# Offsets of split weights in SBUF, PSUM banks cleared by VectorE, and the order and stores at the end of an encoder trunk

## The chip, the cores and the metric

The kernel runs on one core of a Trainium2 chip. The metric is the device time of one execution in microseconds, the median of three runs.

## The reference

One layer of a streaming encoder on x of 256 tokens by 2048 channels, all in float32, with a memory of 256 tokens:

```
h = rms_norm(x, norm_mix_g);  x = x + hybrid_mixer(h, ...)      # w_in: 2048 x 18464, w_out: 2048 x 2048
h = rms_norm(x, norm_x_g);    x = x + cross_attention(h, mem_n, w_xq, w_xkv, w_xo)
h = rms_norm(x, norm_ffn_g);  x = x + square(relu(h @ w_ff1)) @ w_ff2     # 2048 x 8192 and 8192 x 2048
out = rms_norm(x, norm_final_g)
```

The mixer holds two recurrences over chunks of 64 tokens (retention and gated DeltaNet); their arithmetic is small beside the projections, which read 391 MB from HBM in this kernel, scratch included.

## The kernel before

**Products in three parts.** TensorE (PE) multiplies in a short float format (`fp32r`), so each operand is split in two: ACT copies the float32 data into a high part, and DVE subtracts that from the data for a low part. A product of two matrices is high x high + high x low + low x high. Activations stand in tiles `q`, a high and a low half side by side; weights come by DMA into `raw` (1 MB a piece, issued on SP's queue) and are split by `fetch` into `whi` and `wlo` (L93 and L94), 128 x 1024 each, in four buffers.

**Three ways to use them.** `chunk` (token-major projections) loads activations as the stationary operand and streams 512 columns of weights past them (L134 to L136). `blocks` (feature-major projections: the result has channels on the partitions) does the reverse: for each of 16 slices of the contraction, 128 x 128 blocks of `whi` are loaded and the 512 columns of the high and low activations streamed past (L172, one matmul for each of two banks), and then blocks of `wlo`, past which only the 256 columns of high activations are streamed (L174). These four matmuls, two wide and two narrow, are called a pass here. `seven_products` does part of the second MLP product by Strassen's scheme with seven instead of eight products: stationary `q` or `cm` (mixes of hidden activations), streams `sh` and `sl` of 256 columns (mixed weights; L1043 to L1045, 42 matmuls a call, 16 calls: `strassen(q)` for q = 0 to 3 in each of the four blocks `fb` of the MLP). The seven results accumulate over the whole MLP in four PSUM banks `seven`, which `unmix` reads at the end. `thin` is a small form of `blocks`.

**Places in SBUF.** A tile can be used from an offset within its room: `SHIFT` = 48 elements = 192 bytes. In the built program, before and after the change alike, every `q`, `whi`, `wlo`, `sh`, `sl` and `cm` begins 224 bytes past a multiple of 256, so that the offset in the code is the distance, within 256 bytes, between what a matmul streams and what is loaded meanwhile. `chunk` uses offset 0. `blocks` calls `fetch` with `at=SHIFT`, so `whi` and `wlo` both stand at +192. `seven_products` takes its offset from the call: 8 x ((4 fb + q) mod 8) elements, 0, 32, ... 224 bytes, each for two of the 16 calls.

**Order.** The code is written in program order, and a scheduler reorders it by priority: `tc.high_priority(offset=...)` draws a part ahead (fetches by 100000, evacuations by 50000). Each engine then executes its list in order. In the MLP, each `fb` has eight `blocks` (hidden activations, w_ff1), among which `strassen(0)` and `strassen(1)` follow, then three `chunk`s n = 1, 2, 3 (w_ff2), after each of which but the last comes the next `strassen`. `unmix` follows the chunk n = 2 of the last `fb`. The very last chunk is given `hold`: the weights of its two last quarters are fetched early into tiles `q`. Its evacuation `evac_last` normalises each row and stores it.

**The banks `seven`** are opened for accumulation by a matmul with a matrix of zeros, `none` (L1002). The last 128 tokens are written out by four stores of 128 x 512 on SP's queue (L1137); ACT scales the columns c = 0 and 1 (L1136), DVE c = 3 and 2 (L1132, L1134), in the order c = 0, 3, 1, 2.

Of the kernel before, what the change touches and what calls it, by code (L numbers as in the profile page):

```python
# [11 lines left out]
F32R = mybir.dt.float32r  # L12
I32 = mybir.dt.int32
AF = mybir.ActivationFunctionType
# [3 lines left out]
P = 128  # L18
# [15 lines left out]
SHIFT, ROOM = 48, 64  # L34
# [16 lines left out]
def trunk(ctx: ExitStack, tc: tile.TileContext, x, mem, positions, norm_mix_g, w_in, conv_w, gdn_a_log, gdn_dt_bias,  # L51
# [23 lines left out]
    def fetch(pieces, k, n, rush=False, hold=None, at=0):  # L75

        raw = wp.tile([P, k * n], F32, name="raw", tag="raw", bufs=3)
        rv = raw.rearrange("p (k n) -> p k n", k=k)
        with tc.high_priority(offset=100000):
            for off, ap in pieces:  # L80
                src = ap.rearrange("(k p) n -> p k n", p=P)
                for ks in ((slice(0, k // 2), slice(k // 2, k)) if rush else (slice(0, k),)):
                    nc.sync.dma_start(rv[:, ks, off:off + ap.shape[1]], src[:, ks, :])
            got = []
            for i in range(2):
                if hold:
                    both = hold().both
                    hi, lo = (both[:, a:a + 2, :].rearrange("p a s -> p (a s)") for a in (0, 2))
                else:
                    hi, lo = (wp.tile([P, 1024 + ROOM], F32R, name=e, tag=e, bufs=4)[:, at:at + k * n // 2]  # L90
                              for e in ("whi", "wlo"))
                src = raw[:, i * k * n // 2:(i + 1) * k * n // 2]
                act.activation(hi, src, AF.Copy)  # L93
                vec.tensor_sub(lo, src, hi.bitcast(F32))  # L94
                got.append((hi.rearrange("p (k n) -> p k n", n=n), lo.rearrange("p (k n) -> p k n", n=n)))
        return got
# [58 lines left out]
    def cols(w, c0, n=512):  # L155
        return lambda q: [(0, w[q * 512:(q + 1) * 512, c0:c0 + n])]

    def blocks(quads, w, c0, nb, evac, whole=None):

        k = 16 // nb
        ps = stream_ps()
        n = nb * P
        for g in range(KT // k):
            halves = fetch([(0, w[g * k * P:(g + 1) * k * P, c0:c0 + n])], k, n, at=SHIFT)
            for i in range(k):
                kk = g * k + i
                xh, xhl = quads[kk // 4][0][:, kk % 4, :], quads[kk // 4].both[:, kk % 4, :]
                wh, wl = (a[:, i % (k // 2), :] for a in halves[i // (k // 2)])  # L170
                for b in range(nb):
                    pe.matmul(ps[b], wh[:, b * P:(b + 1) * P], xhl, start=kk == 0, stop=False)  # L172
                for b in range(nb):
                    pe.matmul(ps[b][:, :S], wl[:, b * P:(b + 1) * P], xh, start=False, stop=kk == KT - 1)  # L174
        if whole:
            with tc.high_priority(offset=50000):
                o = whole()
                for b in range(nb):
                    act.activation(o[:, b, :], ps[b][:, S:], AF.Copy)
                    vec.tensor_add(o[:, b, :], o[:, b, :], ps[b][:, :S])  # L180
                evac(o)
            return
        for b in range(nb):
            with tc.high_priority(offset=50000):
                o = sm.tile([P, S], F32, name="bo", tag="bo", bufs=2)
                act.activation(o, ps[b][:, S:], AF.Copy)  # L186
                vec.tensor_add(o, o, ps[b][:, :S])  # L187
                evac(b, o)
# [704 lines left out]
    def residual_pass(quads, w, gain, name, loader=None):  # L893
        nxt = []
        acc = xa.tile([P, S], F32, name="acc2", tag="acc2", bufs=2)
        vec.memset(acc, 0.0)
        for b2 in range(8):
            xc = loader(b2) if loader else None
            if b2 % 2 == 0:
                nxt.append(quad_b())  # L900

            def evac(b, ps):
                k = 2 * b2 + b
                vec.tensor_add(rt[:, k, :], ps, xc[:, b, :] if loader else rt[:, k, :])
                g = gains[:, gain + k:gain + k + 1]
                qh, ql = (a[:, k % 4, :] for a in nxt[-1])
                act.activation(qh, rt[:, k, :], AF.Copy, scale=g)
                vec.scalar_tensor_tensor(ql, rt[:, k, :], g, qh.bitcast(F32), op0=ALU.mult, op1=ALU.subtract)
                sq = xa.tile([P, S], F32, name="sq2", tag="sq2", bufs=2)
                act.activation(sq, rt[:, k, :], AF.Square)  # L910
                vec.tensor_add(acc, acc, sq)

            blocks(quads, w, b2 * 256, 2, evac)
        ps = bank()
        for t in range(NT):
            pe.matmul(ps[:, 2 * t:2 * t + 2], acc[:, t * P:(t + 1) * P], ones[:, :2], start=True, stop=True)
        s = sm.tile([P, NT], F32, name=f"{name}_s", tag="rc_s")
        vec.tensor_scalar(s, ps[:, 0:4:2], 1.0 / D, EPS, op0=ALU.mult, op1=ALU.add)
        r = cp.tile([P, NT], F32, name=f"{name}_r")
        rsqrt(r, s)  # L920
        return nxt, r
# [74 lines left out]
        pe.matmul(rps[:, t * P:(t + 1) * P], rstd3[:, t:t + 1].to_broadcast([P, P]), ident, start=True, stop=True)  # L996
    act.activation(rrow3, rps[:, :S], AF.Copy)
    seven = [bank() for _ in range(4)]
    none = fp.tile([P, P], F32R, name="none", bufs=1)
    act.activation(none, ident, AF.Copy, scale=0.0)  # L1000
    for g in range(4):
        pe.matmul(seven[g], none, h3[g].both[:, 0, :], start=True, stop=False)  # L1002

    def mixes(hs):

# [7 lines left out]
        vec.tensor_sub(cm[:, 1], cb, cm[:, 0].bitcast(F32))  # L1013
        return cm

    def seven_products(both, cm, src, last, at):

        raw = wp.tile([P, 2048], F32, name="raw", tag="raw", bufs=3)
        rv = raw.rearrange("p (i x c) -> p i x c", i=2, x=4)
        tt = fp.tile([P, 2, 4, 256], F32, name="tt", tag="tt", bufs=1)  # L1020
        with tc.high_priority(offset=100000):
            nc.sync.dma_start(raw.rearrange("p (k n) -> p k n", k=4), src.rearrange("(k p) n -> p k n", p=P))
            vec.tensor_add(tt[:, :, 0:2, :], rv[:, :, 0:1, :].to_broadcast([P, 2, 2, 256]), rv[:, :, 1:3, :])  # L1023
            vec.tensor_add(tt[:, :, 2, :], tt[:, :, 1, :], rv[:, :, 1, :])
            vec.tensor_add(tt[:, :, 3, :], tt[:, :, 2, :], rv[:, :, 3, :])  # L1025
        for i in range(2):
            with tc.high_priority(offset=100000):
                sh, sl = (fp.tile([P, 7 * 256 + ROOM], F32R, name=n, tag=n, bufs=1)[:, at:at + 7 * 256]
                          .rearrange("p (x c) -> p x c", x=7) for n in ("sh", "sl"))
                for xs, src in ((slice(0, 3), rv[:, i, 1:4, :]), (slice(3, 7), tt[:, i])):  # L1030
                    act.activation(sh[:, xs, :], src, AF.Copy)  # L1031
                    vec.tensor_sub(sl[:, xs, :], src, sh[:, xs, :].bitcast(F32))  # L1032

            def own(k, t):
                return [both[:, 2 * i + k, e * S + t * P:e * S + (t + 1) * P] for e in range(2)]

            def mix(x):
                return [cm[:, e, i, x, :] for e in range(2)]

            for m, (lhs, x) in enumerate(((own(0, 0), 0), (own(1, 0), 2), (mix(3), 1), (own(1, 1), 6), (mix(1), 3),  # L1040
                                          (mix(2), 5), (mix(0), 4))):
                o = seven[m // 2][:, m % 2 * 256:m % 2 * 256 + 256]
                pe.matmul(o, lhs[0], sh[:, x, :], start=False, stop=False)  # L1043
                pe.matmul(o, lhs[0], sl[:, x, :], start=False, stop=False)  # L1044
                pe.matmul(o, lhs[1], sh[:, x, :], start=False, stop=last and i == 1 and (m % 2 == 1 or m == 6))  # L1045

# [21 lines left out]
    for fb in range(4):  # L1068
        hid, mixed = [], []

        def strassen(q):
            seven_products(hid[q].both, mixed[q], w_ff2[0, fb * D + q * 512:fb * D + (q + 1) * 512, 0:512],
                           fb == 3 and q == 3, 8 * ((4 * fb + q) % 8))

        for b2 in range(8):
            if b2 % 2 == 0:
# [13 lines left out]
            blocks(h3, w_ff1[0], fb * D + b2 * 256, 2, evac_h, whole=lambda: fp.tile([P, 2, S], F32, name="ho", tag="ho", bufs=2))  # L1090
            if b2 in (4, 6):
                strassen(b2 // 2 - 2)
        for n in range(1, 4):
            ns = slice(n * 512, (n + 1) * 512)

# [11 lines left out]
            def evac_last(t, ps, c0, c1):  # L1107
# [20 lines left out]
                for c in (0, 3, 1, 2):  # L1128
# [5 lines left out]
                        vec.tensor_scalar(o, o, r, None, op0=ALU.mult)  # L1134
                    else:
                        act.activation(o, o, AF.Copy, scale=r)  # L1136
                    nc.sync.dma_start(out[0, t * P:(t + 1) * P, cs], o)  # L1137

            last = fb == 3 and n == 3
            sums = []  # L1140
            chunk(hid, cols(w_ff2[0, fb * D:(fb + 1) * D, :], n * 512), evac_last if last else evac_o,
                  hold=quad_b if last else None)
            if n < 3:
                strassen(n + 1)
            if fb == 3 and n == 2:
                unmix()
                for t in range(NT):
                    got = res[:, t, 0:512]
                    square_sum(ssq4[:, t, 0:1], got)
                    vec.tensor_mul(got, got, gfin[:, 0:512])  # L1150
# [27 lines left out]
```

## Time and profile before

| | |
|---|---|
| median of three runs | 2068.81 us (2068.43 to 2069.53) |
| the profiled execution's own time | 2068.27 us |
| its span, first to last instruction | 2066.4 us |
| busy: PE, PE's weight loads, DVE, ACT | 2048.0, 1775.5, 1507.3, 1131.0 us |
| mean granted clock of TensorE | 0.999 |
| HBM read, written | 391.19 MB, 15.22 MB |

The busy time of PE is the union of its matmuls, whose ends are modelled: matmuls overlap, so the mean duration of one times their count is far more than that. The weight load of the next matmul (PEld) runs beside the matmul before it.

### The profile page before, as it was taken

The numbers are of one execution on the slowest core, as the hardware profiler recorded it, in microseconds if no ns is written. First come the engines' busy times: TensorE is split into PE (matmuls) and PEld (weight loads), VectorE is DVE, ScalarE is ACT, GpSimd is POOL, SyncE is SP. The second block draws the span as 40 slices with busy tenths as digits, with TensorE's granted clock in tenths as the row PEclk, the third lists the DMA queues.
The fourth block names the chain that finished last, engine by engine and source line by source line (L and its number), as shares of the span: only waits on it lengthen the run. The fifth ranks groups of instructions, "written<-read, shape, count | busy, mean of one in ns | idle before, by whom it ended". The sixth has DMA issues, their size and how long they took to land.

```text
span 2066.4 us, 29100 instructions
## 1 busy us (share of the span) xinstructions
PE 2048.0 (99%) x11244; PEld 1775.5 (86%) x11244; DVE 1507.3 (73%) x2377; ACT 1131.0 (55%) x1670; POOL 28.9 (1%) x37
## 2 busy tenths in 40 slices
PE   8999999999999999999999999999999999999998
PEld 6888888888888888888888898888888888988887
DVE  6775888588957896789667665768757856775875
ACT  7554664556445645565556555566445545554554
POOL 0000000000000000000000000000000000000000
PEclk9999999999999999999999999999999999999999
DMA  8797656575656555655667654665656565656663
GB/s 301 230 315 234 208 186 199 162 212 180 204 174 204 183 193 190 185 190 179 188 196 241 194 178 143 186 196 177 216 186 201 184 203 184 204 186 201 184 206 120
DMA packets 328601, 408.28 MB, mean 198 GB/s; under 512 B 31232, under 2 KB 236560, under 8 KB 328336
## 3 DMA queue, kind: packets, MB, share of 16 engines
q1 hardware_dynamic: 328464, 406.44, 62.0%
q8 instruction: 88, 1.44, 0.3%
q14 instruction: 49, 0.40, 0.1%
HBM read 391.19 MB, written 15.22 MB: 197 GB/s over the span
## 4 chain that ended last, share of the span: by engine, by line
PE 94%; DMA 2%; DVE 2%; SPq 1%; issue 1%; ACT 0%; ACTq 0%; POOLq 0%; POOL 0%; DVEq 0%
PE s L172 34%; PE s L174 17%; PE s L135 12%; PE s L134 12%; PE s L136 12%; PE b L1043 1%; PE b L1045 1%; PE b L1044 1%; PE b L689 1%; DMA raw<-w_ff 1%; DMA xc<-x 1%; PE b L590 1%; DVE wlo L94 1%; PE b L104 0%; PE b L105 0%
## 5 line engine op out<-in xcount | busy, mean ns | idle before, releaser
L94 DVE TENSOR_TENSOR wlo<-raw,whi 128x1024 fp32r<-128x1024 f32 x668 | 815.7, 1223 | 411.4 <-ACT whi L93 404.9
L93 ACT ACTIVATE whi<-raw 128x1024 fp32r<-128x1024 f32 x668 | 706.0, 1060 | 674.7 <-PE s L172 333.4
L172 PE MATMUL s<-q,whi 128*128 128x512 f32 x3072 | 958.5, 392 | 1.4 <-DVE bo L187 1.1
L174 PEld LDWEIGHTS s<-q,wlo 128*128 128x128 f32 x3072 | 575.0, 188 | 123.7
L174 PE MATMUL s<-q,wlo 128*128 128x256 f32 x3072 | 611.1, 279 | 0.0
L172 PEld LDWEIGHTS s<-q,whi 128*128 128x128 f32 x3072 | 468.4, 188 | 4.4 <-DVE bo L187 1.7
L135 PE MATMUL s<-wlo,q 128*128 128x512 f32 x1136 | 443.3, 390 | 1.3 <-DVE wlo L94 1.3
L134 PE MATMUL s<-whi,q 128*128 128x512 f32 x1136 | 442.9, 392 | 0.3 <-ACT whi L93 0.3
L136 PE MATMUL s<-whi,q 128*128 128x512 f32 x1136 | 441.4, 390 | 0.0
L135 PEld LDWEIGHTS s<-wlo,q 128*128 128x128 f32 x1136 | 213.7, 188 | 44.7 <-DVE wlo L94 2.1
L136 PEld LDWEIGHTS s<-whi,q 128*128 128x128 f32 x1136 | 213.3, 188 | 43.1
L134 PEld LDWEIGHTS s<-whi,q 128*128 128x128 f32 x1136 | 213.3, 188 | 42.8 <-ACT whi L93 0.9
L541 DVE SCALAR_TENSOR_TENSOR acc<-bo,cw,acc 128x255 f32<-128x255 f32 (+1 forms) x144 | 61.3, 479 | 3.3 <-ACT acc L538 3.0
L1031 ACT ACTIVATE sh<-raw 128x768 fp32r<-128x768 f32 x32 | 27.1, 847 | 55.3 <-DMA raw<-w_ff 43.1
L187 DVE TENSOR_TENSOR bo<-bo,s 128x256 f32<-128x256 f32 x128 | 47.9, 415 | 0.0
L649 DVE TENSOR_TENSOR pr<-lw,tw 32x31 f32<-32x31 f32 (+15 forms) x124 | 40.2, 324 | 9.7 <-DMA lw<-scr_l 8.2
L651 DVE TENSOR_TENSOR tw<-tw,pr 32x31 f32<-32x31 f32 (+15 forms) x124 | 40.5, 327 | 2.2
L186 ACT ACTIVATE bo<-s 128x256 f32<-128x256 f32 x128 | 41.1, 370 | 0.0
L1023 DVE TENSOR_TENSOR tt<-raw 128x1024 f32<-128x1024 f32 x16 | 19.6, 1225 | 28.8 <-DMA raw<-w_ff 28.8
L1031 ACT ACTIVATE sh<-tt 128x1024 fp32r<-128x1024 f32 x32 | 33.7, 1053 | 11.6 <-DVE tt L1025 11.6
L1032 DVE TENSOR_TENSOR sl<-tt,sh 128x1024 fp32r<-128x1024 f32 x32 | 39.1, 1223 | 0.0
L1044 PE MATMUL b<-sl,cm 128*128 128x256 f32 x128 | 35.7, 281 | 0.0
(361 smaller groups left out, 1593.9 us busy)
## 6 DMA issues: line engine op xcount, KB each, us to landing
raw<-w_in SPq DMA_DIRECT2D x143, 1024.0 KB, 5.3
raw<-w_ff SPq DMA_DIRECT2D x128, 1024.0 KB, 5.8
raw<-w_xkv SPq DMA_DIRECT2D x31, 1024.0 KB, 6.1
raw<-w_out SPq DMA_DIRECT2D x16, 1024.0 KB, 5.6
raw<-w_xq SPq DMA_DIRECT2D x16, 1024.0 KB, 5.4
raw<-w_xo SPq DMA_DIRECT2D x16, 1024.0 KB, 5.4
dec_d<-dec_w SPq DMA_DIRECT2D x8, 384.0 KB, 8.1
dec<-dec_d SPq DMA_DIRECT2D x8, 384.0 KB, 4.4
```

Of the source, the lines that this page charges most:

```text
L93: act.activation(hi, src, AF.Copy)
L94: vec.tensor_sub(lo, src, hi.bitcast(F32))
L134: pe.matmul(o, xh, wh, start=first, stop=False)
L135: pe.matmul(o, xh, wl, start=False, stop=False)
L136: pe.matmul(o, xl, wh, start=False, stop=last)
L172: pe.matmul(ps[b], wh[:, b * P:(b + 1) * P], xhl, start=kk == 0, stop=False)
L174: pe.matmul(ps[b][:, :S], wl[:, b * P:(b + 1) * P], xh, start=False, stop=kk == KT - 1)
L186: act.activation(o, ps[b][:, S:], AF.Copy)
L187: vec.tensor_add(o, o, ps[b][:, :S])
L541: vec.scalar_tensor_tensor(acc[:, d:], ps[:, :S - d], cw[:, j, blk:blk + 1], acc[:, d:], op0=ALU.mult, op1=ALU.add)
L1031: act.activation(sh[:, xs, :], src, AF.Copy)
L1044: pe.matmul(o, lhs[0], sl[:, x, :], start=False, stop=False)
```

## The change

Six edits. (1) In `fetch`, the offset `at` now holds for `whi` only; `wlo` always stands at 0. Only `blocks` gives an offset, so its high weights stay at +192 and its low ones move to 0. (2) `seven_products` uses +192 bytes in every call. (3) The banks `seven` are cleared by four DVE memsets of 128 x 512, and `none`, its ACT copy and its four matmuls go; the first product into each bank opens it. (4) `blocks` takes a parameter `ahead` for the priority of its evacuation; in `residual_pass` the first two of eight get 200000 instead of 50000. (5) In the last `fb`, `strassen(2)` stands before the three chunks and `strassen(3)` after n = 1 (before: after n = 1 and n = 2). (6) The last 128 tokens are written by two stores of 128 x 1024, one on ACT's queue after c = 1, one on SP's after c = 2.

```diff
--- before.py
+++ after.py
@@ -87,8 +87,8 @@
                     both = hold().both
                     hi, lo = (both[:, a:a + 2, :].rearrange("p a s -> p (a s)") for a in (0, 2))
                 else:
-                    hi, lo = (wp.tile([P, 1024 + ROOM], F32R, name=e, tag=e, bufs=4)[:, at:at + k * n // 2]
-                              for e in ("whi", "wlo"))
+                    hi, lo = (wp.tile([P, 1024 + ROOM], F32R, name=e, tag=e, bufs=4)[:, o:o + k * n // 2]
+                              for e, o in (("whi", at), ("wlo", 0)))
                 src = raw[:, i * k * n // 2:(i + 1) * k * n // 2]
                 act.activation(hi, src, AF.Copy)
                 vec.tensor_sub(lo, src, hi.bitcast(F32))
@@ -155,7 +155,7 @@
     def cols(w, c0, n=512):
         return lambda q: [(0, w[q * 512:(q + 1) * 512, c0:c0 + n])]
 
-    def blocks(quads, w, c0, nb, evac, whole=None):
+    def blocks(quads, w, c0, nb, evac, whole=None, ahead=50000):
 
 
 
@@ -181,7 +181,7 @@
                 evac(o)
             return
         for b in range(nb):
-            with tc.high_priority(offset=50000):
+            with tc.high_priority(offset=ahead):
                 o = sm.tile([P, S], F32, name="bo", tag="bo", bufs=2)
                 act.activation(o, ps[b][:, S:], AF.Copy)
                 vec.tensor_add(o, o, ps[b][:, :S])
@@ -910,7 +910,7 @@
                 act.activation(sq, rt[:, k, :], AF.Square)
                 vec.tensor_add(acc, acc, sq)
 
-            blocks(quads, w, b2 * 256, 2, evac)
+            blocks(quads, w, b2 * 256, 2, evac, ahead=50000 if b2 > 1 else 200000)
         ps = bank()
         for t in range(NT):
             pe.matmul(ps[:, 2 * t:2 * t + 2], acc[:, t * P:(t + 1) * P], ones[:, :2], start=True, stop=True)
@@ -996,10 +996,8 @@
         pe.matmul(rps[:, t * P:(t + 1) * P], rstd3[:, t:t + 1].to_broadcast([P, P]), ident, start=True, stop=True)
     act.activation(rrow3, rps[:, :S], AF.Copy)
     seven = [bank() for _ in range(4)]
-    none = fp.tile([P, P], F32R, name="none", bufs=1)
-    act.activation(none, ident, AF.Copy, scale=0.0)
     for g in range(4):
-        pe.matmul(seven[g], none, h3[g].both[:, 0, :], start=True, stop=False)
+        vec.memset(seven[g], 0.0)
 
     def mixes(hs):
 
@@ -1013,7 +1011,7 @@
         vec.tensor_sub(cm[:, 1], cb, cm[:, 0].bitcast(F32))
         return cm
 
-    def seven_products(both, cm, src, last, at):
+    def seven_products(both, cm, src, first, last):
 
         raw = wp.tile([P, 2048], F32, name="raw", tag="raw", bufs=3)
         rv = raw.rearrange("p (i x c) -> p i x c", i=2, x=4)
@@ -1025,7 +1023,7 @@
             vec.tensor_add(tt[:, :, 3, :], tt[:, :, 2, :], rv[:, :, 3, :])
         for i in range(2):
             with tc.high_priority(offset=100000):
-                sh, sl = (fp.tile([P, 7 * 256 + ROOM], F32R, name=n, tag=n, bufs=1)[:, at:at + 7 * 256]
+                sh, sl = (fp.tile([P, 7 * 256 + ROOM], F32R, name=n, tag=n, bufs=1)[:, SHIFT:SHIFT + 7 * 256]
                           .rearrange("p (x c) -> p x c", x=7) for n in ("sh", "sl"))
                 for xs, src in ((slice(0, 3), rv[:, i, 1:4, :]), (slice(3, 7), tt[:, i])):
                     act.activation(sh[:, xs, :], src, AF.Copy)
@@ -1040,7 +1038,7 @@
             for m, (lhs, x) in enumerate(((own(0, 0), 0), (own(1, 0), 2), (mix(3), 1), (own(1, 1), 6), (mix(1), 3),
                                           (mix(2), 5), (mix(0), 4))):
                 o = seven[m // 2][:, m % 2 * 256:m % 2 * 256 + 256]
-                pe.matmul(o, lhs[0], sh[:, x, :], start=False, stop=False)
+                pe.matmul(o, lhs[0], sh[:, x, :], start=first and i == 0 and m % 2 == 0, stop=False)
                 pe.matmul(o, lhs[0], sl[:, x, :], start=False, stop=False)
                 pe.matmul(o, lhs[1], sh[:, x, :], start=False, stop=last and i == 1 and (m % 2 == 1 or m == 6))
 
@@ -1070,7 +1068,7 @@
 
         def strassen(q):
             seven_products(hid[q].both, mixed[q], w_ff2[0, fb * D + q * 512:fb * D + (q + 1) * 512, 0:512],
-                           fb == 3 and q == 3, 8 * ((4 * fb + q) % 8))
+                           fb == 0 and q == 0, fb == 3 and q == 3)
 
         for b2 in range(8):
             if b2 % 2 == 0:
@@ -1090,6 +1088,8 @@
             blocks(h3, w_ff1[0], fb * D + b2 * 256, 2, evac_h, whole=lambda: fp.tile([P, 2, S], F32, name="ho", tag="ho", bufs=2))
             if b2 in (4, 6):
                 strassen(b2 // 2 - 2)
+        if fb == 3:
+            strassen(2)
         for n in range(1, 4):
             ns = slice(n * 512, (n + 1) * 512)
 
@@ -1134,14 +1134,20 @@
                         vec.tensor_scalar(o, o, r, None, op0=ALU.mult)
                     else:
                         act.activation(o, o, AF.Copy, scale=r)
-                    nc.sync.dma_start(out[0, t * P:(t + 1) * P, cs], o)
+                    if not t:
+                        nc.sync.dma_start(out[0, t * P:(t + 1) * P, cs], o)
+                    elif c in (1, 2):
+                        cs = slice(1024 * (c // 2), 1024 * (c // 2) + 1024)
+                        (nc.scalar if c == 1 else nc.sync).dma_start(out[0, t * P:(t + 1) * P, cs], res[:, t, cs])
 
             last = fb == 3 and n == 3
             sums = []
             chunk(hid, cols(w_ff2[0, fb * D:(fb + 1) * D, :], n * 512), evac_last if last else evac_o,
                   hold=quad_b if last else None)
-            if n < 3:
+            if n < 3 and fb < 3:
                 strassen(n + 1)
+            if fb == 3 and n == 1:
+                strassen(3)
             if fb == 3 and n == 2:
                 unmix()
                 for t in range(NT):
```

The order of instructions, at the places where it changes. DVE, at the start of the MLP, where the memsets come in (`wlo` is the split of weights, `n_s` the norm's sum, `ho` the hidden activations as `blocks` leaves them). Before:

```order
L94 TENSOR_TENSOR wlo<-raw,whi 128x1024 x2
L918 TENSOR_SCALAR n_s<-b 128x2
L94 TENSOR_TENSOR wlo<-raw,whi 128x1024 x2
L180 TENSOR_TENSOR ho<-ho,s_13010 128x256
L180 TENSOR_TENSOR ho<-ho,s_13011 128x256
L1082 SCALAR_TENSOR_TENSOR ho<-ho,rrow_12992 128x512
L94 TENSOR_TENSOR wlo<-raw,whi 128x1024
```

and after the change:

```order
L94 TENSOR_TENSOR wlo<-raw,whi 128x1024 x2
L918 TENSOR_SCALAR n_s<-b 128x2
L94 TENSOR_TENSOR wlo<-raw,whi 128x1024
L1000 MEMSET b 128x512 x2
L94 TENSOR_TENSOR wlo<-raw,whi 128x1024
L180 TENSOR_TENSOR ho<-ho,s_13008 128x256
L180 TENSOR_TENSOR ho<-ho,s_13009 128x256
L1000 MEMSET b 128x512 x2
L1080 SCALAR_TENSOR_TENSOR ho<-ho,rrow_12992 128x512
L94 TENSOR_TENSOR wlo<-raw,whi 128x1024
```

The memsets of the four banks stand between two splits of weights and behind the two adds L180; the rest keeps its order (line numbers shift by two).

PE, where the last chunk begins, behind the first half of `strassen(3)`. Before (`s_18726` and `s_18727` are its two banks, `b` in L1045 a bank of `seven`):

```order
L1045 MATMUL b<-sh,cm 128x256
L1043 MATMUL b<-sh,cm 128x256
L1044 MATMUL b<-sl,cm 128x256
L1045 MATMUL b<-sh,cm 128x256
L134 MATMUL s_18726<-whi,q 128x512
L134 MATMUL s_18727<-whi,q 128x256
L135 MATMUL s_18726<-wlo,q 128x512
L136 MATMUL s_18726<-whi,q 128x512
```

After the change the last chunk's banks are `s_18724` and `s_18725` (with `b` for its third part), and the chunk n = 2 accumulates in `s_18556` and `s_18557`:

```order
L136 MATMUL s_18557<-whi,q 128x512
L134 MATMUL s_18556<-whi,q 128x512
L134 MATMUL s_18557<-whi,q 128x512
L134 MATMUL s_18724<-whi,q 128x512
L134 MATMUL s_18725<-whi,q 128x256
L134 MATMUL b<-whi,q 128x256
L135 MATMUL s_18556<-wlo,q 128x512
L136 MATMUL s_18556<-whi,q 128x512
L135 MATMUL s_18557<-wlo,q 128x512
L136 MATMUL s_18557<-whi,q 128x512
L134 MATMUL s_18556<-whi,q 128x512
L135 MATMUL s_18556<-wlo,q 128x512
```

The last chunk's first three matmuls now stand among the last ones of the chunk n = 2, and its first low product (L135 into `s_18724`) ten rows further on; no product by seven is near.

DVE, about the splits of that chunk's weights. Before (`q` is the early part of those weights, `pc` the unmixing):

```order
L94 TENSOR_TENSOR wlo<-raw,whi 128x1024
L94 TENSOR_TENSOR q<-raw,q 128x1024 x2
L1098 TENSOR_TENSOR res<-s_18498,res 128x512
L1098 TENSOR_TENSOR res<-s_18499,res 128x512
L94 TENSOR_TENSOR wlo<-raw,whi 128x1024 x2
L1105 TENSOR_TENSOR res<-res,gfin 128x512
L1032 TENSOR_TENSOR sl<-raw,sh 128x768
```

and after:

```order
L94 TENSOR_TENSOR q<-raw,q 128x1024
L1058 TENSOR_TENSOR pc<-pc 128x256
L1062 TENSOR_TENSOR pc<-pc 128x256
L1061 TENSOR_TENSOR res<-res,pc 128x256
L94 TENSOR_TENSOR q<-raw,q 128x1024
L94 TENSOR_TENSOR wlo<-raw,whi 128x1024
L1059 TENSOR_TENSOR res<-res,pc 128x256
L1063 TENSOR_TENSOR res<-res,pc 128x256
L94 TENSOR_TENSOR wlo<-raw,whi 128x1024 x3
L1098 TENSOR_TENSOR res<-s_18556,res 128x512
L1098 TENSOR_TENSOR res<-s_18557,res 128x512
L94 TENSOR_TENSOR wlo<-raw,whi 128x1024
```

Before, the splits of the last chunk's first weights stand behind the adds L1098 of the chunk n = 2 (`s_18498`, `s_18499`), and the second half of `strassen(3)` and the unmixing further on; now the unmixing and all of those splits but one stand ahead of these adds (`s_18556`, `s_18557`).

SP, the end of its list. Before:

```order
L1022 DMA raw<-w_ff 128x4x512
L83 DMA raw<-w_ff 128x4x512 x4
L1022 DMA raw<-w_ff 128x4x512
L83 DMA raw<-w_ff 128x4x512 x4
L1137 DMA out<-res 128x512 x8
```

and after:

```order
L1020 DMA raw<-w_ff 128x4x512
L83 DMA raw<-w_ff 128x4x512 x4
L1020 DMA raw<-w_ff 128x4x512
L83 DMA raw<-w_ff 128x4x512 x8
L1138 DMA out<-res 128x512 x4
L1141 DMA out<-res 128x1024
```

Of the eight stores the four of the last tokens become one here; the other is the last row of ACT's list. The pieces of w_ff2 for the products by seven (L1022 before, L1020 after) no longer stand between those of the last two chunks (L83).

## Rows read from the trace of the kernel before

**Rows 1.** The page: busy times (part 1) and the costliest group (part 5).
```profile
PE 2048.0 (99%) x11244; PEld 1775.5 (86%) x11244; DVE 1507.3 (73%) x2377; ACT 1131.0 (55%) x1670; POOL 28.9 (1%) x37
...
L172 PE MATMUL s<-q,whi 128*128 128x512 f32 x3072 | 958.5, 392 | 1.4 <-DVE bo L187 1.1
```

**Rows 2.** Waits of PE: engine, tile, line, releaser: us in total, times, longest.
```profile
PE s L135 <- DVE wlo L94: 1.3, 2, 0.7
PE s L172 <- DVE bo L187: 1.1, 1, 1.1
```

**Rows 3.** Windows: stretch, length, busy PE, PEld, DVE, ACT, POOL, clock, DMA share, GB/s.
```profile
1535.00:1589.00 54.00, 54.00 (x315) 47.50 (x314) 40.49 (x50) 31.59 (x40) 0.00 (x0) 1.00 0.63 190
...
2061.80:2064.56 2.76, 0.00 (x0) 0.00 (x0) 0.00 (x0) 0.00 (x0) 0.00 (x0) 0.65 0.97 364
```

**Rows 4.** Timeline of PE, `blocks` in the MLP: start, duration, instruction, count.
```profile
1535.99 0.62 PE L172 MATMUL s<-q,whi 128*128 128x512 f32 x2
1536.45 0.39 PE L174 MATMUL s<-q,wlo 128*128 128x256 f32 x2
1536.68 0.62 PE L172 MATMUL s<-q,whi 128*128 128x512 f32 x2
...
1585.67 0.62 PE L172 MATMUL s<-q,whi 128*128 128x512 f32 x2
```

**Rows 5.** Timeline at the start of the MLP, with idle before and its releaser.
```profile
1373.76 1.23 DVE L94 TENSOR_TENSOR wlo<-raw,whi 128x1024 fp32r<-128x1024 f32 x1 [3.24 <-ACT whi L93]
...
1378.35 1.09 PE L1002 MATMUL b<-q,none 128*128 128x512 f32 x4
...
1379.28 0.28 PE L174 MATMUL s<-q,wlo 128*128 128x256 f32 x1
```

**Rows 6.** Groups by line: busy and mean ns, idle before.
```profile
L662 DVE MEMSET inv<- 128x1024 f32 x4 | 3.6, 912 | 0.6 <-issue 0.6
```

**Rows 7.** Timeline of PE, three stretches of L1043 to L1045: 21, 20, 19 matmuls.
```profile
1415.99 0.28 PE L1043 MATMUL b<-sh,q 128*128 128x256 f32 x1
...
1418.37 0.28 PE L1045 MATMUL b<-sh,cm 128*128 128x256 f32 x1
...
1654.90 0.28 PE L1044 MATMUL b<-sl,q 128*128 128x256 f32 x1
...
1657.14 0.28 PE L1045 MATMUL b<-sh,cm 128*128 128x256 f32 x1
...
1663.46 0.28 PE L1044 MATMUL b<-sl,q 128*128 128x256 f32 x1
...
1665.52 0.28 PE L1045 MATMUL b<-sh,cm 128*128 128x256 f32 x1
```

**Rows 8.** Timeline of PE in one `chunk`: the first and last of 151 matmuls.
```profile
974.84 0.39 PE L134 MATMUL s<-whi,q 128*128 128x512 f32 x1
...
1008.85 0.39 PE L134 MATMUL s<-whi,q 128*128 128x512 f32 x1
```

**Rows 9.** Timeline of PE behind the stall in `residual_pass`.
```profile
1288.87 0.50 PE L172 MATMUL s<-q,whi 128*128 128x512 f32 x1 [1.13 <-DVE bo L187]
...
1290.74 0.40 PE L172 MATMUL s<-q,whi 128*128 128x512 f32 x1
...
1292.86 0.40 PE L172 MATMUL s<-q,whi 128*128 128x512 f32 x1
```

**Rows 10.** Timeline of PE where the last chunk begins.
```profile
2031.50 0.28 PE L1045 MATMUL b<-sh,cm 128*128 128x256 f32 x1
...
2033.78 0.40 PE L136 MATMUL s<-whi,q 128*128 128x512 f32 x1
```

**Rows 11.** Timeline of the last stores: ACT, DVE and SP.
```profile
2060.08 1.33 ACT L1136 ACTIVATE res<-res,r 128x512 f32<-128x512 f32 x2 [1.91 <-POOL r L222]
...
2060.75 0.48 DVE L1134 TENSOR_SCALAR res<-res,r 128x512 f32<-128x512 f32 x1
...
2060.82 1.80 SPq L1137 DMA_DIRECT2D out<-res  x4
```

## Prediction

> **What bounds the kernel now.** I read the page's busy times first [rows 1]: TensorE (PE) is busy 2048.0 us of a span of 2066.4, 99%, while VectorE (DVE) has 73% and ScalarE (ACT) 55%. The list of PE's waits comes next: apart from the first loads at the kernel's start it holds little more than two entries, 1.3 and 1.1 us [rows 2]. So the time is the sum of the distances from one matmul's start to the next, and there are 11,244 of them. An edit can gain in two ways: by shortening that distance in a form that occurs thousands of times, or by removing one of the few waits. The granted clock over a long stretch is 1.00 [rows 3], which is the upper of TensorE's two levels (2.4 GHz), so nothing is to be had from it.
>
> The duration that the page gives for one matmul (392 ns for L172 [rows 1]) overlaps the next and is no price. The price is the difference of starts. In `blocks` 72 passes, each of two 512-wide and two 256-wide matmuls, lie between the starts 1535.99 and 1585.67 [rows 4]: 49.68 / 72 = 690 ns a pass. In the first of them the wide pair takes 0.46 and the narrow pair 0.23. L172 has 3072 matmuls, so there are 3072 / 2 = 1536 passes [rows 1], 1060 us of the span. One nanosecond a pass is 1.5 us.
>
> The sum is made against the profiled execution (span 2066.4, its own time 2068.27). The median of the runs is 0.54 above that and is added at the end. A measurement of this kernel can tell about 0.2%, 4.1 us, from no change.
>
> **The matmuls `none`, now four memsets.** The four L1002 begin at 1378.35 and the next L174 at 1379.28 [rows 5]: PE gets **-0.9** back, since nothing else of PE's stands in that gap. The four DVE MEMSETs have no row of their size. The nearest is a MEMSET of twice the width, 912 ns [rows 6], so about 0.46 each, 1.8 us on DVE. The order of DVE puts them between the L94s around 1373.76, before which DVE idled 3.24 us waiting for ACT [rows 5], and PE waits for DVE nowhere there. Bound if that cover is gone: +1.8. I take 0.
>
> **The MLP's products by seven (L1043 to L1045).** 16 calls of 42 matmuls make 672. Two calls (fb 1 and fb 3, q 2) are at 192 bytes already; 14 x 42 = 588 change. The distance of starts comes from the first and last matmul of undisturbed stretches [rows 7]: 2.38 / 20 = 119.0 ns at offset 0 (the stretch from 1415.99), and at 192 bytes 2.24 / 19 = 117.9 (from 1654.90) and 2.06 / 18 = 114.4 (from 1663.46). By the first stretch at 192 the change is 1.1 x 588 = 0.65 us, by the mean of both 2.85 x 588 = 1.7. I take **-1.0**, nearer the first, since one and the same offset gave both. Bounds: 0 (the offsets between may be as good as 192 on average), and 4.6 x 588 = -2.7 (all as from 1663.46).
>
> **The blocks' low weights, from +192 to 0 bytes.** In each pass one wide and one narrow matmul now have, beside their stream of activations, the load of a low weight at the activations' own place in 256 bytes. No row shows `blocks` so; three neighbours bound it. `chunk` has all at offset 0: 150 starts from 974.84 to 1008.85 [rows 8], 226.7 ns each, so 453.5 a wide pair against about 455.5 here (690 less the narrow pair, 0.23 to 0.24). Its stream and its stationary operand are the other way round, though. The narrow form at offset 0 in the seven products has 119.0, against 117 here: that alone would be +2. And the regular pass is no minimum: two starts at 226.7 and two at the 114.4 of 1663.46 would be 682, -8 ns. Dearer patterns exist too: from 1290.74 to 1292.86, after a stall had put wide and narrow matmuls in turn, six pairs take 2.12 us [rows 9], 353 ns a pair or 707 a pass, +17. That these differ at all, for the same shapes at the same clock, shows that the places of load and stream in SBUF matter. I take the chunk's rate for both wide starts, since a lag left by one load is carried to the next start, and leave the narrow pair: -2 ns x 1536 = **-3.1**. The bounds are -8 x 1536 = -12 and +17 x 1536 = +26.
>
> The Trainium skill, "TensorE: Matmul & The Clock Gate", Part 2, step 1, says that PE has two independent SBUF read ports, so that loading the next weights takes nothing from the running matmul. By that rule no offset could matter, and both offset terms would be 0. The 114.4 against 119.0 ns for one shape [rows 7] speaks against it, if not by how much `blocks` moves.
>
> **The order at the end of the MLP.** Before, the chunk n = 3 of fb 3 starts behind the first half of `strassen(3)`: from that half's last L1045 at 2031.50 to the first L136 at 2033.78 [rows 10] are 2.28 us, where the four starts on the way (narrow, wide, narrow, wide) would take 115 + 227 + 115 + 227 ns = 0.69. That is 1.6 us lost on the splits of the last weights; the waits listed for L135 [rows 2] are shorter, since a matmul's modelled end still counts as busy. DVE did two adds L1098 before that split, and what stands next on PE is that chunk's. Afterwards `strassen(2)` runs before the chunks and `strassen(3)` after n = 1; the last chunk's first rows stand among the last matmuls of chunk n = 2, so PE has something to do while the split ends, and DVE's unmixing lies earlier beside matmuls. **-1.6**; bound 0, if DVE's three L94 in a row behind the unmixing come as late as before. What is late next is then the end itself, which does not move against PE: evac_last and its chain are the same.
>
> **`ahead` = 200000** for the first two blocks of residual_pass. On ACT, DVE and PE the order up to the MLP is the same as before, so nothing moves. The stall of 1.13 us at 1288.87 [rows 9] stays. **0**; bound -1.1, if it went after all.
>
> **The last stores.** Before, SP issues four stores of 256 KB from 2060.82 on [rows 11] and the DMA engines are 97% busy from 2061.80 to 2064.56 [rows 3]: 2.76 us for 1 MB, 0.98 after the first issue. Now SP's store of 512 KB needs both of DVE's pieces, the second of which ends at 2060.75 + 0.48 = 2061.23, and ACT's needs both of ACT's, 2060.08 + 1.33 = 2061.41 [rows 11]. The first issue is 0.45 later, and the same bytes follow at the same rate: **+0.45**. Bounds 0 (larger pieces win it back) and +0.8.
>
> **Sum.** -0.9 - 1.0 - 3.1 - 1.6 + 0 + 0.45 = -6.2: 2062.1 for an execution such as the profiled one, 2062.6 for the median.
>
> **The rivals.**
> (1) The offsets change nothing. For it: two of the three stretches [rows 7] lie within 1.1 ns of each other though their offsets differ. Against it: the third, at 114.4. The skill's rule above is this rival's. The rest is -0.9 - 1.6 + 0.45 = -2.1: about **2066.8**, not to be told from no change.
> (2) Slower: mixing a load at +192 with one at 0 breaks the pattern that returns every pass, and `blocks` falls into a dearer one, as after the stall [rows 9]. Its place is all of the 1536 passes, its price up to +17 ns. The other terms are -3.1, so it decides from (4.1 + 3.1) / 1536 = 4.7 ns a pass (695); at the full price the sum is -3.1 + 26 = +23, **2092**. Against it: these passes alternate wide and narrow, which the change doesn't do.
> (3) Much faster: the pass falls to the 682 of the best neighbours: -3.1 - 12, **2053.5**. For it: both parts of 682 were seen at this clock. Against it: neither in `blocks`.
> (4) The offsets act as forecast but the wait at the last chunk stays, because the last weights are split as late as before: **2064.2**. For it: DVE's order still has splits of those weights among the last things before the adds L1098. Against it: PE has other matmuls to go on with.
>
> **How the numbers follow.** Forecast, a pass 0.6 to 6 ns shorter: 0.38. Rival 1: 0.24. Rival 2: 0.20, of which 0.17 beyond +0.2%. Rival 3: 0.12. Rival 4: 0.06, half of it within 0.2%. Faster: 0.38 + 0.12 + 0.03 = 0.53; same: 0.24 + 0.03 + 0.03 = 0.30; slower 0.17. The likeliest case alone is 2056.5 to 2064.8. The range for 8 in 10 takes in rival 1, rival 3 but for a pass below 678, and of rival 2 what costs up to +5 ns a pass: 2048 to 2074.
>
> **What would show it.** In `blocks`, 72 passes in 49.5 us instead of 49.68. In the seven products, 117 ns at every call. No L1002; DVE's memsets without a wait of PE beside them. At the last chunk, no wait for wlo. Stores: first packets about 2.2 us after r. The prediction is wrong if the pass goes to 695 or more, or if a new wait of PE for DVE appears where the memsets or the unmixing stand.

## The result, and the profile after

The changed kernel takes 2076.68 us (2075.87 to 2078.29, six runs) against 2068.7 before: a ratio on record of 1.0042, interval 1.0032 to 1.0052 (the two medians alone give 1.0039). It is slower by 8.0 us, and outside the forecast range. The profiled execution spans 2074.7 us, 8.3 more than before.

The page after, busy times and the group of L172 (as [rows 1]):

```profile
PE 2057.3 (99%) x11240; PEld 1778.6 (86%) x11240; DVE 1509.9 (73%) x2381; ACT 1132.0 (55%) x1669; POOL 26.9 (1%) x37
...
L172 PE MATMUL s<-q,whi 128*128 128x512 f32 x3072 | 967.6, 395 | 1.2 <-DVE bo L187 1.1
```

PE is as full as before and has 9.3 us more work, though four matmuls fewer. Its waits (as [rows 2]) have not grown, and the one for `wlo` that is left stands at 30.67, near the kernel's start:

```profile
PE s L172 <- DVE bo L187: 1.1, 1, 1.1
PE s L135 <- DVE wlo L94: 0.5, 1, 0.5
```

So the loss is in the distances between starts. The timeline of PE in `blocks`, at the place of [rows 4]:

```profile
1543.87 0.63 PE L172 MATMUL s<-q,whi 128*128 128x512 f32 x2
...
1592.87 0.39 PE L172 MATMUL s<-q,whi 128*128 128x512 f32 x1
```

These are 70 passes in 49.00 us, 700 ns each, every one alike, where before passes of 688 and 692 ns took turns. Elsewhere in the same trace `blocks` runs in other patterns. The timeline of PE in the mixer's projections, and then at the start of the MLP:

```profile
120.18 0.62 PE L172 MATMUL s<-q,whi 128*128 128x512 f32 x2
...
120.87 0.64 PE L172 MATMUL s<-q,whi 128*128 128x512 f32 x2
...
121.58 0.62 PE L172 MATMUL s<-q,whi 128*128 128x512 f32 x2
...
122.28 0.62 PE L172 MATMUL s<-q,whi 128*128 128x512 f32 x2
...
122.98 0.62 PE L172 MATMUL s<-q,whi 128*128 128x512 f32 x2
...
125.77 0.62 PE L172 MATMUL s<-q,whi 128*128 128x512 f32 x2
...
1390.07 0.64 PE L172 MATMUL s<-q,whi 128*128 128x512 f32 x2
...
1390.78 0.64 PE L172 MATMUL s<-q,whi 128*128 128x512 f32 x2
...
1391.48 0.64 PE L172 MATMUL s<-q,whi 128*128 128x512 f32 x2
...
1392.19 0.64 PE L172 MATMUL s<-q,whi 128*128 128x512 f32 x2
```

From 120.18 on, eight passes take 5.59 us, 699 ns each; to the nanosecond, passes of 690, 710, 695 and 698 repeat, 698 on average. From 1390.07 on, three take 2.12, 707 each. Once entered, a pattern holds for the rest of the stretch.

Adding up all distances of starts in both traces by form gives the whole difference. What exceeds an undisturbed distance is put down as stalls, and `none` stands for its four matmuls:

| | before, us | after, us | difference |
|---|---|---|---|
| `blocks`, wide matmuls (3072) | 704.3 | 714.0 | +9.7 |
| `blocks`, narrow (3072) | 356.8 | 360.0 | +3.2 |
| products by seven (672) | 79.6 | 78.2 | -1.4 |
| `none` | 0.9 | 0 | -0.9 |
| stalls | 12.4 | 10.1 | -2.2 |
| `chunk` and all the rest of PE | 901.6 | 901.3 | -0.3 |
| last matmul's start to the end of the span | 8.4 | 8.7 | +0.3 |

The sum is +8.4, against 8.3 in the spans.

The other edits, in the timeline after. DVE's memsets, the products by seven in two stretches, the start of the last chunk, and the last stores:

```profile
1379.19 1.02 DVE L1000 MEMSET b<- 128x512 f32 x2 [1.39 <-ACT res L988]
...
1383.05 1.03 DVE L1000 MEMSET b<- 128x512 f32 x2
...
1488.48 0.28 PE L1042 MATMUL b<-sl,q 128*128 128x256 f32 x1
...
1490.72 0.28 PE L1043 MATMUL b<-sh,cm 128*128 128x256 f32 x1
...
1497.03 0.28 PE L1042 MATMUL b<-sl,q 128*128 128x256 f32 x1
...
1499.09 0.28 PE L1043 MATMUL b<-sh,cm 128*128 128x256 f32 x1
...
2040.93 0.96 PE L134 MATMUL s<-whi,q 128*128 128x512 f32 x4
2041.72 0.28 PE L134 MATMUL b<-whi,q 128*128 128x256 f32 x1
2041.84 0.40 PE L135 MATMUL s<-wlo,q 128*128 128x512 f32 x1
...
2068.08 1.33 ACT L1136 ACTIVATE res<-res,r 128x512 f32<-128x512 f32 x2 [1.92 <-POOL r L222]
...
2069.25 0.33 SPq L1141 DMA_DIRECT2D out<-res  x1
2069.44 0.37 ACTq L1141 DMA_DIRECT2D out<-res  x1
```

Two memsets in a row take 1.02 (485 ns is the duration of one, the rest is the gap between them), and no wait of PE stands there. The two stretches of products by seven have 20 and 19 matmuls: 2.24 / 19 = 117.9 and 2.06 / 18 = 114.4 ns, the same two values as at 192 bytes in [rows 7]. At the last chunk PE goes on without a pause where [rows 10] had lost 1.6 us. The first store's issue is 1.17 after the last factor r is there (before 0.74, [rows 11]). The windows of the stores themselves, as in [rows 3]:

```profile
2070.10:2072.70 2.60, 0.00 (x0) 0.00 (x0) 0.00 (x0) 0.00 (x0) 0.00 (x0) 0.50 1.01 399
```

1 MB now goes in 2.60 us instead of 2.76.

### The profile page after: what moved, and what is told of

It reads as the page before. It is cut to its first block, busy times and chain, and to the rows that moved or that the text cites. A ratio compares the mean times of both kernels' runs of the same rounds, so it can differ in the third digit from the quotient of the medians.

```text
span 2074.7 us, 29089 instructions
## 1 busy us (share of the span) xinstructions
PE 2057.3 (99%) x11240; PEld 1778.6 (86%) x11240; DVE 1509.9 (73%) x2381; ACT 1132.0 (55%) x1669; POOL 26.9 (1%) x37
## 4 chain that ended last, share of the span: by engine, by line
PE 98%; DMA 1%; SPq 1%; issue 0%; DVE 0%; ACT 0%; POOLq 0%; POOL 0%; DVEq 0%; ACTq 0%
PE s L172 34%; PE s L174 17%; PE s L135 12%; PE s L134 12%; PE s L136 12%; PE b L1041 1%; PE b L1042 1%; PE b L1043 1%; PE b L689 1%; DMA xc<-x 1%; PE b L590 1%; PE b L104 0%; PE b L105 0%; PE b L106 0%; SPq L290 0%
## 5 line engine op out<-in xcount | busy, mean ns | idle before, releaser
L172 PE MATMUL s<-q,whi 128*128 128x512 f32 x3072 | 967.6, 395 | 1.2 <-DVE bo L187 1.1
L172 PEld LDWEIGHTS s<-q,whi 128*128 128x128 f32 x3072 | 473.5, 189 | 4.0 <-DVE bo L187 1.3
L135 PE MATMUL s<-wlo,q 128*128 128x512 f32 x1136 | 443.7, 391 | 0.5 <-DVE wlo L94 0.5
L136 PE MATMUL s<-whi,q 128*128 128x512 f32 x1136 | 441.7, 390 | 0.0
L135 PEld LDWEIGHTS s<-wlo,q 128*128 128x128 f32 x1136 | 213.8, 188 | 43.2 <-DVE wlo L94 0.9
L136 PEld LDWEIGHTS s<-whi,q 128*128 128x128 f32 x1136 | 213.5, 188 | 42.8
L1043 PE MATMUL b<-sh,cm 128*128 128x256 f32 x128 | 35.6, 279 | 0.0
```

The source lines that it names most:

```text
L135: pe.matmul(o, xh, wl, start=False, stop=False)
L136: pe.matmul(o, xl, wh, start=False, stop=last)
```

## The experiments

The theory after this reading: the offset of the low weights alone made `blocks` slower, by 12.9 us, and the rest of the change gained about 4.5. The rival: the new order (memsets, priorities, the last products) shifted where `blocks` enters, and so its patterns, and the offset is innocent.

**e1_low_back**: the changed kernel, low weights back at +192.

```diff
-                              for e, o in (("whi", at), ("wlo", 0)))
+                              for e, o in (("whi", at), ("wlo", at)))
```

> The changed kernel with the low weights of blocks back at +192 bytes; all its other edits stay. Theory (the offset of the low weights alone made blocks slower, all other terms came as summed): the wide and narrow matmuls fall back by 12.9 us, so 2076.7 - 12.9 = about 2063.8, 0.998 of the kernel before, and a pass of 690 to 692 ns. Rival (the new order, memsets or priorities put blocks into a dearer pattern): 2074 to 2077, pass about 700 ns.

Measured: 2065.74 us, 0.9989 of before (0.998 to 0.9997), 10.9 under the changed kernel. The timeline of PE in `blocks`:

```profile
1535.62 0.62 PE L172 MATMUL s<-q,whi 128*128 128x512 f32 x2
...
1583.92 0.39 PE L172 MATMUL s<-q,whi 128*128 128x512 f32 x1
```

70 passes in 48.30 us are 690 ns again. The theory's 2063.8 is missed by 1.9, and in the profiled execution the waits of PE show most of it: L172 waits for `bo` twice, 2.5 us in all, not once.

```profile
PE s L172 <- DVE bo L187: 2.5, 2, 1.4
```

The second wait, at 1084.4, is in the first `residual_pass`. Edit 4 sets a priority there, but up to the MLP every engine's order is that of before. By the starts the wait cost 0.3 us in the profile before, 1.5 here, and nothing in the changed kernel. What differs is a load: ahead of the evacuation for which PE waits, ACT has to split `vr`, a piece of the attention's values, and waits for its DMA. The timeline of ACT, first before, then here:

```profile
1081.22 1.06 ACT L100 ACTIVATE vvh<-vr 128x1024 fp32r<-128x1024 f32 x1 [0.90 <-DMA vr<-vv_d]
...
1082.21 1.06 ACT L100 ACTIVATE vvh<-vr 128x1024 fp32r<-128x1024 f32 x1 [2.23 <-DMA vr<-vv_d]
```

Why that load lands at different times from run to run isn't shown.

**e2_low_only**: the kernel before, with the low weights alone at 0.

```diff
-                    hi, lo = (...[:, at:at + k * n // 2]
-                              for e in ("whi", "wlo"))          # both at +192
+                    hi, lo = (...[:, o:o + k * n // 2]
+                              for e, o in (("whi", at), ("wlo", 0)))
```

> The kernel before with the low weights of blocks at 0 bytes and nothing else changed; every engine's order is that of before. Theory: 2068.7 + 12.9 = about 2081.6, 1.006 of the kernel before, with the passes at 695 to 710 ns as in the changed kernel. Rival (order and priorities): 2068 to 2070.

Measured: 2080.8 us, 1.0056 of before (1.0041 to 1.0072), with wide matmuls 8.8 and narrow ones 3.3 us dearer in the sum of starts. PE in `blocks`, same place:

```profile
1545.78 0.62 PE L172 MATMUL s<-q,whi 128*128 128x512 f32 x2
...
1594.78 0.39 PE L172 MATMUL s<-q,whi 128*128 128x512 f32 x1
```

70 passes in 49.00, 700 ns each, although every engine's order is that of before. The rival falls: the one edit alone costs 12.2 us of time, about all of the 12.9 that the sum of starts put on `blocks`.

**p1_shift_all**: the changed kernel, everything in SBUF 64 bytes lower.

```diff
-    cp.tile([P, 56], F32, name="pad0")
+    cp.tile([P, 40], F32, name="pad0")
```

> The changed kernel with the first pad 64 bytes shorter, so that every tile in SBUF moves by 64 bytes and all distances between tiles stay; every engine's order is the same. Theory (distances decide): 2076 to 2078 as the changed kernel, pass about 700 ns. Rival (the place itself decides, for instance against what DMA, ScalarE and VectorE write): another time, by 3 us or more.

Measured: 2077.47 us, 1.004 of before (1.0025 to 1.0056); the stretch has 700 ns a pass again:

```profile
1543.64 0.62 PE L172 MATMUL s<-q,whi 128*128 128x512 f32 x2
...
1592.64 0.62 PE L172 MATMUL s<-q,whi 128*128 128x512 f32 x2
```

Behind its first four passes, each of the 96 calls of `blocks` has the same mean pass here as in the changed kernel to within 1 ns, so the patterns return from run to run. What counts is how the operands stand to each other, not where they all stand (for a shift of 64 bytes).

**s1_offsets**: one trace with 16 pairs of offsets.

```diff
+TABLE = [...]        # 96 pairs of offsets, one for each call of blocks
...
-            halves = fetch([...], k, n, at=SHIFT)
+            halves = fetch([...], k, n, at=at)         # at = TABLE[number of the call]
```

> The changed kernel, but each of the 96 calls of blocks takes its own pair of offsets (high, low) from the 16 pairs of 0, 64, 128 and 192 bytes, six calls each in scrambled order, so that one trace shows the pass for each pair. Theory A (the distance between a load and the stream beside it decides, each matmul for itself): the pass is the sum of a part for the high and a part for the low offset; with 0 for high and 192 for low as dear as the reverse, and 0 with 0 dearer still, over 705 ns. Theory B (mixing two distances is what costs): 0 with 0 and all other equal pairs come near 690, all unequal ones 698 to 710. If offsets don't decide, all 16 lie within 3 ns.

Measured: the mean pass in ns, from the starts of six calls (86 to 95 undisturbed passes each):

```
high \ low      0       64      128     192
     0        696.6   700.0   699.9   694.1
    64        710.7   694.4   700.0   694.2
   128        706.0   705.2   698.5   703.8
   192        700.8   702.2   702.5   692.1
```

The pair of before is the cheapest of the sixteen, and the pair of the change costs 8.7 ns more. Theory A is wrong: 0 with 0 is cheaper than 192 with 0, and the reverse pair, 0 with 192, has 694.1. Theory B holds only on average (the diagonal has 695.4, the rest 701.6): two unequal pairs in the last column have 694, and 128 with 128 has 698.5. The patterns can be read directly. Timeline of PE, 16 passes at 192 with 192 from 862.78, then 15 of 64 with 0 from 873.84:

```profile
862.78 0.63 PE L177 MATMUL s<-q,whi 128*128 128x512 f32 x2
...
873.84 0.62 PE L177 MATMUL s<-q,whi 128*128 128x512 f32 x2
...
884.51 0.63 PE L177 MATMUL s<-q,whi 128*128 128x512 f32 x2
```

11.06 / 16 = 691 and 10.67 / 15 = 711 ns. The pair 192 with 0 settles in different patterns in different calls. In the call from 693.67 it ends at 706 to 707:

```profile
693.67 0.62 PE L177 MATMUL s<-q,whi 128*128 128x512 f32 x2
...
694.37 0.64 PE L177 MATMUL s<-q,whi 128*128 128x512 f32 x2
...
704.26 0.64 PE L177 MATMUL s<-q,whi 128*128 128x512 f32 x2
```

14 passes in 9.89 us, 706 each; in a call from 1543.97 the same pair has 700 from its third pass on, in one from 1309.28 690, 710, 695 and 698 in turn. At 192 with 192 every call falls, after at most five other passes, into 687 to 688 and 692 to 693 in turn.

**s2_offsets**: sixteen other pairs, and pairs of offsets in `chunk`.

```diff
-                halves = fetch(pieces_of(q), 4, 512, rush=...)
+                halves = fetch(pieces_of(q), 4, 512, rush=..., at=ct)     # ct = CTABLE[number of the chunk]
```

> The changed kernel with sixteen other pairs of offsets in blocks (high, low; six calls each): equal pairs at 32, 96, 160 and 224 bytes, low at 192 with high at 32, 96, 160, 224, and six more with an odd multiple of 32, beside 192 with 192; and in chunk, too, the 16 pairs of 0 to 192 bytes, two calls or so each. Theory B (equal distances of high and low are cheap, unequal ones dear): the equal pairs at 690 to 699, the unequal ones at 700 and more. If the low offset of 192 by itself is what is cheap: 692 to 696 with every high offset. In chunk 0 with 0 gives 227.5 ns a wide matmul; nothing says that it is the best, and any pair under 226.5 would be worth 3 us and more.

Measured: 192 with 192 again the cheapest, 692.5; 224 with 0 has 693.6 and 224 with 224 693.8; the other 13 lie from 697.7 to 706.5. Equal pairs at 32, 96 and 160 have 702 to 704, and 96 with 192 has 706, so neither equality nor the low offset of 192 is the rule. In `chunk` 0 with 0 is the cheapest of 16: three matmuls take 682.8 ns, with the other pairs 687.6 to 702.0. No gain was found there. The kernel with both tables takes 2092.0 us in its one run, so the dearer pairs in `chunk` reach the time too.

**s3_fine**: pairs some bytes away from 192. Its edit is another table, and four stores.

> Four stores as before, and sixteen pairs of offsets in blocks close to 192 bytes: equal pairs at 176, 184, 188, 196, 200, 208, 216 and 240 bytes, and 192 with a neighbour 4 or 8 bytes away. If the distance acts in steps of 32 bytes, the pairs from 192 to 216 act as 192 with 192 (687 and 693 ns in turn) and those from 176 to 188 as 160 with 160 (704 on average). If it acts byte by byte, each has its own value, and one may be under 690.

Measured: 192 with 192 has 691.4. High 4 bytes lower gives 696.6, high 4 bytes higher 696.4, low 4 bytes lower 700.1, low 4 bytes higher 703.1, and high 8 bytes lower 694.4; all other equal pairs from 176 to 240 lie between 698.7 and 701.2. Steps of 32 bytes are thereby ruled out: the distance acts at every 4 bytes tried. 192 with 192 is a narrow best value, and none is under 690. I had no theory that gives it.

**e3_four_stores**: e1 with the old stores; and **e4_best**, the same kernel timed.

```diff
-                    if not t:
-                        nc.sync.dma_start(out[0, t * P:(t + 1) * P, cs], o)
-                    elif c in (1, 2):
-                        cs = slice(1024 * (c // 2), 1024 * (c // 2) + 1024)
-                        (nc.scalar if c == 1 else nc.sync).dma_start(out[0, t * P:(t + 1) * P, cs], res[:, t, cs])
+                    nc.sync.dma_start(out[0, t * P:(t + 1) * P, cs], o)
```

> The changed kernel with the low weights back at +192 and the last tokens stored in four pieces on SP's queue as before. From the last matmul's start to the end of the span: 8.4 us as in the kernel before, against 8.7 with the two stores; all else as with the low weights back, span about 2062.3 to 2063.5.

Measured: span 2063.3, as expected; its last L136 begins at 2054.93, 8.4 before the end, as in the kernel before. With two stores (the changed kernel and e1) it is 8.7.

> The changed kernel without the two edits that cost time: low weights at +192 again, four stores. By the sums of matmul distances 2068.7 - 0.9 (none) - 1.5 (products by seven) - 1.5 to 1.7 (last chunk) = 2064.6 to 2064.8, ratio 0.998; a rival, that the run with two stores was helped by them, would give 2065.7 or more.

Measured: 2065.07 us, 0.9982 of before (0.9973 to 0.9991). That is 0.3 over the range expected and 0.6 under the rival's. It is the fastest version found, 11.6 us under the changed kernel and 3.6 under the kernel before. The wait at 1084.7 takes 0.7 us more here than before, and the last chunk's gain is partly spent on it.

**e5_order_back**: e4 with the old order at the end.

```diff
-        if fb == 3:
-            strassen(2)
...
-            if n < 3 and fb < 3:
+            if n < 3:
                 strassen(n + 1)
-            if fb == 3 and n == 1:
-                strassen(3)
```

> The version with the low weights back and four stores, and the old order at the end (strassen after the chunks n = 1 and n = 2 of the last fb too). Theory: PE's stall at the start of the last chunk returns, 1.3 to 1.6 us, with waits of L134 for ScalarE or L135 for VectorE near 2030; all else as in that version, span 2064.5 to 2065.

Measured: span 2064.7, 1.5 more than e4, and the wait is back. Timeline of PE:

```profile
2030.34 0.28 PE L1043 MATMUL b<-sh,cm 128*128 128x256 f32 x1
2030.55 0.62 PE L134 MATMUL s<-whi,q 128*128 128x512 f32 x2
2031.82 0.50 PE L135 MATMUL s<-wlo,q 128*128 128x512 f32 x1 [0.64 <-DVE wlo L94]
2032.15 0.40 PE L136 MATMUL s<-whi,q 128*128 128x512 f32 x1
```

From 2030.34 to 2032.15 are 1.81 us instead of 0.69: 1.1 lost here, 1.6 before. The other 0.4 is the wait at 1084 again. The order is worth 1.1 to 1.6.

**e6_seven_back**: e4 with the old offsets of the products by seven.

```diff
-                sh, sl = (fp.tile([...])[:, SHIFT:SHIFT + 7 * 256]
+                sh, sl = (fp.tile([...])[:, at:at + 7 * 256]          # at = 8 * ((4 * fb + q) % 8)
```

> The same version with the old offsets of the products by seven (0 to 224 bytes in turn), order as in the change. Theory: the 672 matmuls take 1.5 us more (118.4 instead of 116.2 ns each on average), at offset 0 120 ns in a steady row, at 192 either 113 to 114 or 117 to 118; span 2064.5 to 2065.

Measured: the 672 matmuls take 79.5 us against 78.1 in e4, 1.5 more, as expected; span 2064.6. A steady row of 120 ns at offset 0 stands in one of the four stretches there; the others average 118.7 to 119.3.

## Why the prediction was wrong, by its own steps

**What bounds the kernel**: right. PE's starts are the time, and behind the first loads no wait cost over 1.6 us.

**The matmuls `none` and the memsets**: right. -0.9 on PE; 0.49 a memset against an estimate of 0.46, and the first of them waited 1.39 us for ACT on DVE, with no wait of PE beside it.

**The products by seven**: right in mechanism, a little under-sized: -1.4 in place of -1.0 (e6: 1.5). All stretches now have one of the two averages seen at 192 before, about 114.4 or 117.9, and the mean of both was the better estimate.

**The blocks' low weights**: the step that failed. I took "the chunk's rate for both wide starts" and wrote -2 ns a pass; the trace has +8.9 (690.5 to 699.4 on the average of undisturbed passes), +12.9 us over all starts in place of -3.1, and e1 and e2 put it on this edit alone. The four distances of a pass went from 227.8, 230.5, 116.7, 115.5 to 230.5, 234.5, 116.3, 118.2 ns. The second, beside which the first low weight is now loaded at 0, grew most. But the third, beside which the other low weight is loaded, did not grow, and the fourth and the first, whose loads had not moved, did: no distance goes by the load beside it alone. The two wide ones came to 465 together, not to the chunk's 453.5. The error was to take a price from neighbours of another form: `chunk` is cheapest at 0 with 0 (s2), but that says nothing of `blocks`, where the cheapest of all pairs tried is the one that was in place (s1 to s3). The trace of before gave two hints: the regular pass fell back into one and the same pattern from every entry, and the other pattern in `blocks` [rows 9] was dearer. That one came with another order of the four matmuls, so by itself it showed nothing of the offsets.

**Rival 2** was the side that came true: `blocks` falls into dearer patterns, at about half its full price and over the 4.7 ns that it asked for. I held against it that the dear pattern of [rows 9] has an order which the change doesn't bring; that doesn't matter, since e2 has the loss with the order of before. Its reason, the mixing of two offsets, is not the rule either: the mixed pairs 0 with 192 and 224 with 0 have 694, the equal pairs at 32, 96 and 160 have 702 to 704. **Rival 3**, a pass of 682, has no support: of the 46 pairs in the three tables none averages under 691.

**Rival 1**, and the rule that it rested on (the Trainium skill, "TensorE: Matmul & The Clock Gate", Part 2: separate read ports for weights and stream, so that a load takes no SBUF read bandwidth from the running matmul): the trace disagrees with what was drawn from it, that no offset could matter. With the same shapes and the same clock, passes of 691 and 711 ns stand one behind the other in s1, by the offsets alone. What inside the chip makes it so isn't shown here.

**The order at the end**: right, -1.6 expected, all of it gone in the timeline after, 1.1 lost again in e5; so rival 4 falls. **`ahead`**: right, the wait of 1.1 us is still there. **The stores**: right in sign, over-sized: +0.3 instead of +0.45, as 0.43 of later issue was partly won back by 2.60 us instead of 2.76 for the transfer (e3).

Without `blocks` the sum had -3.1; the trace shows -4.5 in those parts, stalls elsewhere included.

**What stays open**: why 192 with 192 is best, and whether an untried pair, or another order of the four matmuls of a pass, comes under 690.

## What to carry to other kernels

Where PE is full, weigh the start-to-start distance of each form of matmul, and treat operand offsets as something to be measured in the form itself: a table of offsets, one pair for each call of the helper, compares sixteen of them in one trace. A pattern that returns from every entry, and that no pair of a table undercuts, is worth leaving alone. When six edits go together and one is repeated 1536 times, price that one from a run of its own before the sum.

## What was not expected of the hardware

A shift of 4 bytes of one operand in SBUF moves a pass of four matmuls by 5 to 12 ns (s3: 691.4 against 696.4 to 703.1). In most undisturbed stretches PE falls into exact patterns of one to five passes, the same to within a nanosecond in call after call. For some offsets there are several (690 to 710, 700, or 707 at 192 with 0). Which of them a call enters returns from run to run (p1); what picks it isn't shown.
